# Two matmul accumulator rings re-cut in a two-block transformer kernel, and the side work issued between weight pairs

## The chip, the cores and the metric

The kernel runs as one program on one core of a Trainium2 chip. The metric is the device time of one execution in microseconds (us). Lower is better.

## The reference, cut to what matters

Two transformer blocks follow each other on 512 tokens of width 1024, in float32. The change touches the MLP of the first block, the modulation that is computed beside it for the second block, and, through a shared constant, the start of the MLP of the second block.

```python
# first block
hn = rmsnorm(x, mlp_norm_g)
hid = jnp.square(jax.nn.relu(hn @ w_up))          # 512x1024 @ 1024x4096
x = x + hid @ w_down                              # 512x4096 @ 4096x1024

# second block: six modulation rows of 1024 for x, the first two for ctx too
mod_x = jax.nn.silu(c) @ w_mod + b_mod            # 1x1024 @ 1024x6144
mod_c = jax.nn.silu(c_ctx) @ w_mod + b_mod
h_c = rmsnorm(ctx, g_pre_mix) * (1 + csc1) + csh1
...
y_x = (relu(modulate(x, ...) @ w_mlp_in) ** 2) @ w_mlp_out
```

## The kernel before, in words

**Products.** Every float32 product is made of three matmuls (`mm3`, lines 156 to 158): both factors are split into a high and a low part, and high by high, high by low and low by high are summed in one PSUM bank. ACT makes the high part of a weight tile (L151, a copy of 128x1024), DVE the low part (L152, a subtraction). A weight tile lands in one of two `raw` buffers, and its two parts stand in one of five buffers of each kind.

**The first block's MLP** (`mlp`, called with the name `m1`) runs over four groups of eight hidden slices. In a group, `up` makes eight slices `m1u0` to `m1u31`: 24 matmuls of 512 columns into one bank of the ring `s`, then ACT's relu (L847) and DVE's square (L848) read that bank, and the result is split again. For the first `NSP` = 5 slices the ring has `MORE` banks besides its own, and their matmuls go in two halves of 256 columns. After the eight slices, `token_major` makes the second product for each half of the output columns. Its weights come in four pairs (`m1d000` is group 0, half 0, pair 0), and each of the four token tiles has an accumulator of the ring `a`. DVE adds the finished accumulator to the residual (L987, `xa`). One half is 4 token tiles x 4 pairs x 6 matmuls. The loops stand as pair outside, token tile inside, but the ring `a` has three banks, so the fourth token tile is taken up when the first one's bank has been read.

**Modulation** (`mods`) is a generator whose steps are taken out by `extra`, two at a call. A step of the first kind loads 128x1024 of the modulation weights (`mod`, L897, on SP's queue, two buffers) and adds it, scaled, to an accumulator on DVE (`macc`, L901 and L903): two additions a load for the first two of six column blocks, one for the others. After the eight loads of a block come `MLAG` empty steps, and then a step per row that splits the accumulator, sums it over partitions with four matmuls (`mp`) and writes the row to DRAM. `extra` is called after each `up` and, in the second product, ahead of the addition of each token tile. In the last group its first call takes out what is left and prepares the normalized `ctx`.

**The order** of instructions on each engine is set when the kernel is built. A scheduler goes through the program with estimates of its own, takes the earliest instruction in program order whose inputs and buffers are ready in them, and writes one fixed list for each engine. On the chip each engine works its list in that order. So program order is a priority, and an engine can wait at the head of its list for data that came later than the estimate.

**After the first MLP** `kc` and `vc` are made from `ctx` with the rings `s` and `a`.

**The second block's MLP** (`mlp_seven`, name `m2`) sets `self.rings["s"] = s_banks + list(MORE)` with `s_banks` = `S2` = (5, 6, 7), for its first five slices too. Their first 256 columns need the token tiles 0 and 1 of the normalized input (`h2T`), the other 256 the tiles 2 and 3. `ps` gives out the banks of a ring in turn.

Of the kernel before, what the change touches and what calls it, by code (L numbers as in the profile page):

```python
# [19 lines left out]
NT = SEQ // P  # L20
KC = D // P
FF = 4 * D
NJ = FF // P
# [62 lines left out]
C1 = 0  # L86
KPG = (1, 3)
NSP = 5
MORE = (0, 1)
EARLY = (2, 1)  # L90
A1 = (0, 1, 2)
XR = (3, 5, 7)
# [7 lines left out]
DT = False  # L100
# [6 lines left out]
RB = 1.5  # L107
PBUF = 3
RATIO = 1.6
MLAG = 4  # L110
MRAW = 4
RB_2 = 6
SIZES_2 = (8, 8, 8, 4, 4)
# [20 lines left out]
class Build:  # L134
# [656 lines left out]
                evac(half, t, acc)  # L791
            turns[t], self.last_turn = self.last_turn, None

    def token_major(self, name, nk, weights, moving, evac, in_turn, nt=NT):


        accs = {}

        def part(t, kp, wh, wl):
            if t not in accs:  # L800
                accs[t] = self.ps("a", f"{name}_{t}")
            cols = slice(t * P, (t + 1) * P)
            for i in range(2):
                k = 2 * kp + i
                m = moving(k)
                self.mm3(accs[t], m[:, 0, cols], m[:, 1, cols], wh[:, i, :], wl[:, i, :], k == 0, k == nk - 1)
            if k == nk - 1:
                evac(t, accs[t])

        if in_turn:  # L810
            tiles = [weights(kp) for kp in range(nk // 2)]
            turns = {}
            for t in range(nt):
                for kp in range(nk // 2):

                    behind = turns.get(t - 2) if kp == KB else None
                    with self.tc.issue_after(behind.ins) if behind else nullcontext():
                        part(t, kp, *tiles[kp])
                turns[t], self.last_turn = self.last_turn, None
        else:  # L820
            for kp in range(nk // 2):
                wh, wl = weights(kp)
                for t in range(nt):
                    part(t, kp, wh, wl)

    def mlp(self, hT, w1, w2, evac, extra, name, G=8):

        nc = self.nc
        ac = nc.scalar.activation
        hq = {}  # L830

        def up(j):
            wh, wl = self.weights(f"{name}u{j}", [(0, self.kview(w1, 0, KC, j * P, P))], KC, P)
            acc = self.ps("s", f"{name}up{j}")
            nsp = 2 if j < NSP else 1
            w = SEQ // nsp
            if j % 4 == 0:
                hq[j // 4] = self.hquad(f"{name}hid{j // 4}")
            qd = hq[j // 4]
            for sp in range(nsp):  # L840
                cols = slice(sp * w, (sp + 1) * w)
                for k in range(KC):
                    hqd = hT[k // 4]
                    self.mm3(acc[:, cols], wh[:, k, :], wl[:, k, :], hqd[:, k % 4, 0, cols], hqd[:, k % 4, 1, cols], k == 0, k == KC - 1)
            r = self.ep.tile([P, SEQ], F32, tag="relu", name=f"{name}re{j}", bufs=2)
            s = self.ep.tile([P, SEQ], F32, tag="sqr", name=f"{name}sq{j}", bufs=2)
            ac(out=r, in_=acc, func=AF.Relu)  # L847
            nc.vector.scalar_tensor_tensor(out=s, in0=acc, scalar=0.0, in1=r, op0=ALU.max, op1=ALU.mult)  # L848
            self.split(qd[:, j % 4, 0, :], qd[:, j % 4, 1, :], s)

        s_banks = self.rings["s"]
        self.rings["s"] = s_banks + list(MORE)
        for g in range(NJ // G):
            for j in range(g * G, (g + 1) * G):
                if j == NSP:
                    self.rings["s"] = s_banks
                up(j)
                extra(g)
            for half in range(2):
                def evac_(t, acc):  # L860
                    extra(g)
                    evac(g, half, t, acc)
                self.token_major(f"{name}d{g}{half}", G,
                                 lambda q: self.weights(f"{name}d{g}{half}{q}", [(0, self.kview(w2, g * G + 2 * q, 2, half * 512, 512))], 2, 512),
                                 lambda i: hq[(g * G + i) // 4][:, i % 4], evac_, DT or (g == NJ // G - 1 and half == 1))

    def hquad(self, name):

# [5 lines left out]
    def mods(self):  # L874
# [18 lines left out]
        for cb in range(6):  # L893
# [12 lines left out]

            for _ in range(MLAG):
                yield
# [25 lines left out]
    def dense_one(self):  # L934
        nc, a = self.nc, self.a
        ac = nc.scalar.activation
        x = [self.xp.tile([P, D], F32, tag=f"x{t}", name=f"xa{t}") for t in range(NT)]
        for t in range(NT):
            nc.gpsimd.dma_start(out=x[t], in_=a["x"][0, t * P:(t + 1) * P, :])
        g = self.gp.tile([P, 2, D], F32, tag="g", name="g_mlp")  # L940
        nc.gpsimd.dma_start(out=g[:, 0, :], in_=a["mlp_norm_g"].partition_broadcast(P))
        hT = [self.quad(f"hT{i}") for i in range(2)]

        r2 = self.xc.tile([P, NT], F32, name="r2")

        def evac1(half, t, acc):
            cols = slice(half * 512, half * 512 + 512)
            nc.vector.tensor_tensor(out=x[t][:, cols], in0=acc, in1=x[t][:, cols], op=ALU.add)
            xg = self.ep.tile([P, D], F32, tag="xr", name=f"xg{half}{t}", bufs=2)
            (nc.vector if half else nc.gpsimd).tensor_tensor(out=xg[:, cols], in0=x[t][:, cols], in1=g[:, 0, cols], op=ALU.mult)  # L950
            self.split_T(xg, hT, t, f"n2_{t}", (half,))
            if half == 1:
                self.inv_rms(x[t], r2, t, f"r2_{t}", self.ep.tile([P, D], F32, tag="xr", name=f"xs{t}", bufs=2))
                nc.gpsimd.tensor_tensor(out=r2[:, t:t + 1], in0=r2[:, t:t + 1], in1=r2[:, t:t + 1], op=ALU.mult)
        self.out_proj(a["w_out"], self.mixT, evac1, "o1")

        self.turned_in = self.last_split
        self.banks(a=(0, 1, 2), t=(3, 4), s=(5, 6, 7))

        self.kc = self.xc.tile([P, 4, 2, 256], F32R, name="kc")  # L960
        self.vc = self.xc.tile([P, 2, 2, 512], F32R, name="vc")
        gen = self.mods()
        hcq = []
        seen = set()

        def extra(grp):
            next(gen, None)
            if grp == 3 and 3 not in seen:
                seen.add(3)
                for _ in gen:  # L970
                    pass

                hcq.append(self.ep.tile([P, 8, 2, 256], F32R, tag="xquad", name="hcT", bufs=1))
                hcT = [hcq[0][:, 0:4], hcq[0][:, 4:8]]
                gc = self.columns("g_ctx", (6, 7))
                for t in range(2):
                    cx = self.raw(f"ctx{t}")
                    nc.sync.dma_start(out=cx, in_=a["ctx_2"][0, t * P:(t + 1) * P, :])
                    self.mod_T(cx, gc, hcT, t, f"nc_{t}")
            else:  # L980
                next(gen, None)
        hxT = []
        gx = []

        def evac2(grp, half, t, acc):
            cols = slice(half * 512, half * 512 + 512)
            nc.vector.scalar_tensor_tensor(out=x[t][:, cols], in0=acc, scalar=r2[:, t:t + 1], in1=x[t][:, cols],  # L987
                                           op0=ALU.mult, op1=ALU.add)
            if grp == NJ // 8 - 1 and half == 1:
                if t == 0:  # L990
                    gx.append(self.columns("g_mod1", (0, 1)))
                    hxT.extend(self.quad(f"hxT{i}") for i in range(2))
                nc.gpsimd.dma_start(out=self.xspill[t * P:(t + 1) * P, :], in_=x[t])
                self.mod_T(x[t], gx[0], hxT, t, f"n3_{t}")
        self.mlp(hT, a["w_up"], a["w_down"], evac2, extra, "m1")


        w_in = a["w_in_2"][0]
        hc = hcq[0]
        for i in range(4):  # L1000
            wh, wl = self.weights(f"wkc{i}", [(0, self.kview(w_in, 0, KC, 1024 + i * P, P))], KC, P)
            acc = self.ps("s", f"kc{i}")
            for k in range(KC):
                self.mm3(acc[:, 0:256], wh[:, k, :], wl[:, k, :], hc[:, k, 0, :], hc[:, k, 1, :], k == 0, k == KC - 1)
            self.split(self.kc[:, i, 0], self.kc[:, i, 1], acc[:, 0:256])
        self.early = {(kind, 0): self.weights_two(kind, 0) for kind in EARLY}
        self.token_major("vc", KC, lambda kp: self.weights(f"wvc{kp}", [(0, self.kview(w_in, 2 * kp, 2, 1536, 512))], 2, 512),
                         lambda k: hc[:, k], lambda t, acc: self.split(self.vc[:, t, 0], self.vc[:, t, 1], acc), False, 2)
        return hxT
# [549 lines left out]
```

## Time and profile before

| | |
|---|---|
| median of 3 runs | 1251.21 us (1248.91 to 1252.83) |
| the profiled execution | 1258.43 us, of which the span of instructions is 1256.6 us |
| TensorE (PE) busy | 1210.2 us, 96% of the span |
| VectorE (DVE) busy | 836.8 us, 67% |
| ScalarE (ACT) busy | 593.8 us, 47% |
| mean granted TensorE clock | 0.989 of full speed |

PE is the engine that is nearly always at work, so a change can gain only where PE waits, where its clock is granted at half, or by fewer matmuls. The first block's MLP lies between 278 and 659 us of the span, the start of the second block's MLP at 903 to 940 us.

### The profile page before, as it was taken

Reading aid. Unit: us, or ns where it says so; the run is one execution under the profiler, and the core shown is the slowest. Engines: PE = TensorE matmul, PEld = TensorE weight load, DVE = VectorE, ACT = ScalarE, POOL = GpSimd, SP = SyncE. Lnnn points to the kernel's source line nnn. Section 1 sums busy time; section 2 is a strip of 40 time slices with the busy share of each in tenths; the row PEclk is TensorE's granted clock in tenths of the full one; section 3 lists DMA queues with packets and bytes.
Section 4 is the critical chain, followed back from the end, with each engine's and each line's share of the span. In section 5 each row is a group of like instructions: output and inputs, shape, how many; then the busy total and the mean of one; then the engine's idle time right before and its main releaser. Section 6 shows DMA issues by size and latency. Waiting matters only on the chain. (4 is left out here: it accounts for less than half of the span.)

```text
span 1256.6 us, 16978 instructions
## 1 busy us (share of the span) xinstructions
PE 1210.2 (96%) x6304; PEld 1012.7 (81%) x6304; DVE 836.8 (67%) x1469; ACT 593.8 (47%) x1103; POOL 232.6 (19%) x316
## 2 busy tenths in 40 slices
PE   7898999999999999999999999999999999999997
PEld 6898888789777878888889878777798888888775
DVE  3698776558978758346356557574768568578675
ACT  5576655443324214225245546463666454453442
POOL 2787552220001000000013224130300000000000
PEclk9899999999999999999999999999999999999999
DMA  6222222336658657134145311306554525426331
GB/s 165 64 52 54 66 63 68 101 101 185 201 186 236 214 154 223 62 118 135 67 150 159 85 51 53 102 26 212 157 167 145 164 90 173 146 89 191 106 101 67
DMA packets 154154, 155.42 MB, mean 124 GB/s; under 512 B 14489, under 2 KB 115624, under 8 KB 154072
## 3 DMA queue, kind: packets, MB, share of 16 engines
q1 hardware_dynamic: 149096, 143.08, 37.7%
q0 software_dynamic: 4400, 10.22, 2.8%
q8 instruction: 49, 0.80, 0.3%
q10 hardware_dynamic: 576, 1.05, 0.2%
q14 instruction: 33, 0.27, 0.1%
HBM read 147.96 MB, written 6.36 MB: 123 GB/s over the span
## 5 line engine op out<-in xcount | busy, mean ns | idle before, releaser
L903 DVE SCALAR_TENSOR_TENSOR macc<-mod,silu_c,macc 128x1024 f32<-128x1024 f32 x56 | 70.9, 1279 | 18.3 <-DMA mod<-in_w_mod_dram 18.2
L1461 POOL TENSOR_TENSOR ss<-ss,nhalf 128x1 f32<-128x1 f32 x4 | 2.9, 736 | 335.6 <-DVE ss L1460 335.6
L1313 DVE TENSOR_TENSOR m2d<-m2d,m2d 128x1024 f32<-128x1024 f32 x28 | 34.2, 1222 | 22.8 <-DMA m2d<-in_w_mlp_out_dram 22.6
L928 POOL DMA_DIRECT2D modrows<-mrow x8 | 3.9, 492 | 220.0 <-DVE mrow L926 143.0
L987 DVE SCALAR_TENSOR_TENSOR xa<-m1d,r,xa 128x512 f32<-128x512 f32 x32 | 23.7, 747 | 30.5 <-PE m1d L158 30.5
L151 ACT ACTIVATE m1hid<-m1sq 128x512 fp32r<-128x512 f32 x32 | 20.1, 629 | 40.2 <-DVE m1sq L848 40.1
L152 DVE TENSOR_TENSOR npl<-t,nph 128x512 fp32r<-128x512 f32 x32 | 21.8, 683 | 17.1 <-ACT nph L151 17.0
L185 POOL TENSOR_SCALAR w<-w,g_attn 128x384 f32<-128x384 f32 x20 | 26.1, 1314 | 9.1 <-DMA w<-in_w_in_dram 4.3
L152 DVE TENSOR_TENSOR m1hid<-m1sq,m1hid 128x512 fp32r<-128x512 f32 x32 | 22.0, 687 | 8.4 <-ACT m1hid L151 8.4
L687 DVE TENSOR_REDUCE mb<-sb 128x1 f32<-128x128 f32 (+3 forms) x32 | 15.6, 486 | 16.9 <-PE sb L684 16.8
L1127 ACT ACTIVATE p<-s,m 128x512 f32<-128x512 f32 x32 | 21.9, 687 | 5.6 <-DVE m L1125 5.5
L689 ACT ACTIVATE pb<-sb,mb 128x128 f32<-128x128 f32 (+3 forms) x32 | 16.8, 526 | 16.1 <-DVE mb L687 15.8
L198 POOL TENSOR_SCALAR p<-p,d 128x512 f32<-128x512 f32 x8 | 14.0, 1753 | 53.9 <-DVE d L1128 28.5
L1081 POOL TENSOR_TENSOR tb<-G,nam 128x256 f32<-128x256 f32 x24 | 18.8, 816 | 22.8 <-DVE m L1121 12.3
L151 ACT ACTIVATE nph<-t 128x512 fp32r<-128x512 f32 x32 | 19.0, 595 | 8.1 <-PE t L1138 7.7
L156 PE MATMUL pj<-w_0h,xnT 128*128 128x384 f32 (+1 forms) x48 | 18.1, 377 | 4.9 <-ACT pjs L411 3.7
L848 DVE SCALAR_TENSOR_TENSOR m1sq<-m1up,m1re 128x512 f32<-128x512 f32 x32 | 21.9, 683 | 0.0
L1339 DVE TENSOR_TENSOR y<-m2p,y 128x512 f32<-128x512 f32 x32 | 21.0, 684 | 0.6 <-PE m2p L158 0.6
L1278 ACT ACTIVATE m2sq<-m2up 128x512 f32<-128x512 f32 x32 | 18.6, 581 | 5.3 <-PE m2up L158 5.3
L1280 ACT ACTIVATE m2sq<-m2sq 128x512 f32<-128x512 f32 x32 | 20.2, 632 | 0.9
L151 ACT ACTIVATE pbh<-tb 128x128 fp32r<-128x128 f32 (+3 forms) x32 | 13.8, 434 | 14.5 <-PE tb L707 14.4
L847 ACT ACTIVATE m1re<-m1up 128x512 f32<-128x512 f32 x32 | 18.6, 581 | 3.7 <-PE m1up L158 3.6
(2045 smaller groups left out, 4596.6 us busy)
## 6 DMA issues: line engine op xcount, KB each, us to landing
m2d<-in_w_mlp_out_dram SPq DMA_DIRECT2D x53, 512.0 KB, 3.7
mod<-in_w_mod_dram SPq DMA_DIRECT2D x48, 512.0 KB, 4.2
m1u<-in_w_up_dram SPq DMA_DIRECT2D x32, 512.0 KB, 4.5
m1d<-in_w_down_dram SPq DMA_DIRECT2D x32, 512.0 KB, 4.5
m2u<-in_w_mlp_in_dram SPq DMA_DIRECT2D x32, 512.0 KB, 4.2
w<-in_w_in_dram SPq DMA_DIRECT2D x16, 512.0 KB, 4.0
w<-in_w_in_dram SPq DMA_DIRECT2D x48, 128.0 KB, 2.6
o1w<-in_w_out_dram SPq DMA_DIRECT2D x8, 512.0 KB, 3.8
```

What stands on the lines that cost most here:

```text
L151: self.nc.scalar.activation(out=hi, in_=src, func=AF.Copy)
L152: self.last_split = (eng or self.nc.vector).tensor_tensor(out=lo, in0=src, in1=hi.bitcast(F32), op=ALU.subtract)
L185: eng.tensor_scalar(out=rv[:, i], in0=rv[:, i], scalar1=g, scalar2=None, op0=ALU.mult)
L847: ac(out=r, in_=acc, func=AF.Relu)
L848: nc.vector.scalar_tensor_tensor(out=s, in0=acc, scalar=0.0, in1=r, op0=ALU.max, op1=ALU.mult)
L903: nc.vector.scalar_tensor_tensor(out=accs[s], in0=rw, scalar=sc[:, s, k:k + 1], in1=accs[s], op0=ALU.mult, op1=ALU.add)
L987: nc.vector.scalar_tensor_tensor(out=x[t][:, cols], in0=acc, scalar=r2[:, t:t + 1], in1=x[t][:, cols], op0=ALU.mult, op1=ALU.add)
L1081: nc.gpsimd.tensor_tensor(out=tb[:, h, y], in0=G[:, h, ::-1, o:o + 32][:, :, ::-1], in1=nam[:, y, :].unsqueeze(1).to_broadcast([P, 8, 32]) ...
L1127: ac(out=pr, in_=s, func=AF.Exp, bias=m[:, 2:3], accum_out=den[:, 0:1])
L1280: ac(out=s, in_=s, func=AF.Square)
L1313: tt(out=o, in0=x, in1=z, op=ALU.subtract)
L1339: tt(out=Y[n][tau], in0=acc, in1=Y[n][tau], op=ALU.add)
```

## The change

The ring `a` gets a fourth bank, 5, during the first MLP, and the ring `s` keeps two, 6 and 7. `MORE` becomes (5, 0, 1), so that the first five slices of the first MLP still have five banks. The rings are set back after the MLP. `extra` is called after each weight pair of the second product and no longer ahead of each token tile's addition, and it takes two steps and one step in turn. `MLAG` goes from 4 to 3. The preparation of `ctx` moves to the call of the last group at which the generator has run out.

```diff
-MORE = (0, 1)
+MORE = (5, 0, 1)
...
-MLAG = 4
+MLAG = 3
...
-    def token_major(self, name, nk, weights, moving, evac, in_turn, nt=NT):
+    def token_major(self, name, nk, weights, moving, evac, in_turn, nt=NT, hook=lambda: None):
...
                 for t in range(nt):
                     part(t, kp, wh, wl)
+                hook()
...
             for half in range(2):
-                def evac_(t, acc):
-                    extra(g)
-                    evac(g, half, t, acc)
                 self.token_major(f"{name}d{g}{half}", G,
                                  lambda q: self.weights(f"{name}d{g}{half}{q}", [(0, self.kview(w2, g * G + 2 * q, 2, half * 512, 512))], 2, 512),
-                                 lambda i: hq[(g * G + i) // 4][:, i % 4], evac_, DT or (g == NJ // G - 1 and half == 1))
+                                 lambda i: hq[(g * G + i) // 4][:, i % 4], lambda t, acc: evac(g, half, t, acc),
+                                 DT or (g == NJ // G - 1 and half == 1), hook=lambda: extra(g))
...
-        self.banks(a=(0, 1, 2), t=(3, 4), s=(5, 6, 7))
+        self.banks(a=(0, 1, 2, 5), t=(3, 4), s=(6, 7))
...
-        seen = set()
+        calls = [0]
 
         def extra(grp):
-            next(gen, None)
-            if grp == 3 and 3 not in seen:
-                seen.add(3)
-                for _ in gen:
-                    pass
+
+            calls[0] += 1
+            for _ in range(1 + calls[0] % 2):
+                more = next(gen, "done") != "done"
+            if grp == 3 and not more and not hcq:
 
                 hcq.append(self.ep.tile([P, 8, 2, 256], F32R, tag="xquad", name="hcT", bufs=1))
...
                     self.mod_T(cx, gc, hcT, t, f"nc_{t}")
-            else:
-                next(gen, None)
...
         self.mlp(hT, a["w_up"], a["w_down"], evac2, extra, "m1")
+        self.banks(a=(0, 1, 2), t=(3, 4), s=(5, 6, 7))
```

## Rows read from the trace of the kernel before

**Rows 1.** The page, busy time of each engine: us, share of the span, instructions.
```profile
PE 1210.2 (96%) x6304; PEld 1012.7 (81%) x6304; DVE 836.8 (67%) x1469; ACT 593.8 (47%) x1103; POOL 232.6 (19%) x316
```
**Rows 2.** Waits of PE, 270 to 700: total us, times, longest.
```profile
PE m1d L156 <- DVE xa L987: 4.9, 3, 2.4
PE m1up L158 <- DVE m1u8l L152: 1.9, 1, 1.9
```
**Rows 3.** Timeline of PE, 344 to 444: start, us, what, [idle before].
```profile
344.16 0.50 PE L156 MATMUL m1d<-m1d000h,m1hid 128*128 128x512 f32 x1 [0.97 <-DVE xa L987]
...
369.25 0.50 PE L156 MATMUL m1d<-m1d010h,m1hid 128*128 128x512 f32 x1 [1.50 <-DVE xa L987]
...
440.15 0.40 PE L158 MATMUL m1d<-m1d103h,m1hid 128*128 128x512 f32 x1
442.96 0.68 PE L156 MATMUL m1d<-m1d100h,m1hid 128*128 128x512 f32 x1 [2.41 <-DVE xa L987]
443.44 0.63 PE L157 MATMUL m1d<-m1d100l,m1hid 128*128 128x512 f32 x1
```
**Rows 4.** Windows: busy us (x) of PE, PEld, DVE, ACT, POOL; PEclk, DMA, GB/s.
```profile
440.50:444.30 3.80, 1.39 (x5) 1.06 (x5) 2.91 (x3) 0.00 (x0) 0.00 (x0) 0.84 0.61 174
904.00:908.50 4.50, 2.61 (x18) 2.61 (x18) 4.33 (x7) 2.12 (x8) 3.66 (x7) 0.87 0.69 198
```
**Rows 5.** Timeline of DVE, 440 to 449.
```profile
440.96 1.28 DVE L903 SCALAR_TENSOR_TENSOR macc<-mod,silu_c,macc 128x1024 f32<-128x1024 f32 x1 [1.64 <-DMA mod<-in_w_mod_dram]
442.16 0.74 DVE L987 SCALAR_TENSOR_TENSOR xa<-m1d,r,xa 128x512 f32<-128x512 f32 x1
...
447.48 0.75 DVE L987 SCALAR_TENSOR_TENSOR xa<-m1d,r,xa 128x512 f32<-128x512 f32 x1
```
**Rows 6.** Tiles macc and mod: durations ns min/median/max, first and last start.
```profile
L903 DVE SCALAR_TENSOR_TENSOR macc<-mod,silu_c,macc x56: 1262/1282/1293, 287.5 to 501.2; 128x1024 f32<-128x1024 f32 x56
...
L897 SPq DMA_DIRECT2D mod<-in_w_mod_dram x48: 327/340/441, 240.3 to 495.9; - x48
```
**Rows 7.** The same windows, over slices of groups 0 and 1.
```profile
290.54:325.46 34.92, 34.92 (x223) 31.57 (x222) 32.94 (x36) 13.38 (x19) 0.48 (x1) 1.00 0.58 180
...
378.85:423.70 44.85, 44.85 (x193) 36.40 (x194) 37.52 (x41) 18.31 (x24) 6.21 (x11) 1.00 0.80 243
```
**Rows 8.** Timeline of PE: the last matmul of slices 13 and 21.
```profile
412.19 0.39 PE L158 MATMUL m1up<-hT,m1u13l 128*128 128x512 f32 x1
...
507.68 0.39 PE L158 MATMUL m1up<-hT,m1u21l 128*128 128x512 f32 x1
507.91 0.40 PE L156 MATMUL m1up<-hT,m1u22h 128*128 128x512 f32 x1
```
**Rows 9.** Timeline of DVE: the square that frees the banks of the same slices.
```profile
421.02 0.68 DVE L848 SCALAR_TENSOR_TENSOR m1sq<-m1up,m1re 128x512 f32<-128x512 f32 x1
...
510.12 0.68 DVE L848 SCALAR_TENSOR_TENSOR m1sq<-m1up,m1re 128x512 f32<-128x512 f32 x1
```
**Rows 10.** Timeline of ACT, 418 to 420.
```profile
418.78 1.06 ACT L151 ACTIVATE m1d102h<-m1d 128x1024 fp32r<-128x1024 f32 x1 [4.17 <-DMA m1d<-in_w_down_dram]
```
**Rows 11.** Timeline of PE, 655: the first `kc` matmul.
```profile
655.32 0.28 PE L156 MATMUL kc<-hcT,wkc0h 128*128 128x256 f32 x1
```
**Rows 12.** Timeline of PE, 905 to 924: the start of the second MLP.
```profile
905.89 0.39 PE L157 MATMUL m2up<-h2T,m2u1h 128*128 128x256 f32 x1 [1.89 <-DVE h2T L152]
...
917.79 1.03 PE L220 MATMUL n_3t<-ident,n_3x 128*128 128x128 f32 x8
...
923.64 0.28 PE L156 MATMUL m2up<-h2T,m2u4h 128*128 128x256 f32 x1
923.76 0.28 PE L157 MATMUL m2up<-h2T,m2u0h 128*128 128x256 f32 x1
```
**Rows 13.** Timeline of DVE, 914 to 922: the input of token tile 3.
```profile
914.63 0.74 DVE L236 TENSOR_SCALAR n_3x<-xb,ssx 128x1024 f32<-128x1024 f32 x1
...
920.62 1.29 DVE L152 TENSOR_TENSOR h2T<-n_3v,h2T 128x512 fp32r<-128x512 f32 x2 [0.40 <-ACT h2T L151]
```

## The prediction

> **What bounds the kernel now.** I read the page first: PE is busy for 96% of the span and the next engine, DVE, for 67% [rows 1]. So time can come only from PE's idle stretches, its half-clock stretches, or PE work saved; the change saves no PE work. Next I read PE's own waits in the stretch of the first MLP [rows 2]. There are two kinds: three waits of 4.9 us for the addition `xa` of a token tile, and one of 1.9 us for the low part of a weight tile, `m1u8l`. The timeline shows where the three are [rows 3]: always at the first `m1d` matmul of a half's fourth token tile, which takes the bank of the first tile. The first tile's last matmul lies 12 matmuls ahead of that point, about 437.4 for the third wait, and its addition ends at 442.90 [rows 5]: 5.5 us later, though the addition takes 0.74. What stands before it on DVE is a modulation step, itself waiting 1.64 us for its load [rows 5]. In program order two such steps stand ahead of each addition, so they go first, and DVE works its list in order.
>
> The wait for `m1u8l` has the same root. As the fourth token tile runs after the other three, it needs all four weight pairs again, so four of the five weight buffers stay taken until the half ends, and the next slices' weights are split late.
>
> **What can be won.** The page's idle times begin at a matmul's end, and matmuls overlap: one of 512 columns starts 0.23 us after the one before [rows 8], though each is shown with 0.40. Start to start the third wait is 442.96 - 440.15 - 0.23 = 2.58 us where 2.41 is shown. So I add 0.17 to each of the four: 6.8 + 0.7 = 7.5 us. After the third wait the granted clock is 0.84 over 3.8 us [rows 4], so part of it is at 1.2 GHz, and the matmuls follow at 0.48 and about 0.43 us instead of 0.23 [rows 3]; six of them make 1.2 us. In all 8.7 us can be won, from nothing (the waits only move) to all of it.
>
> **Part 1: four banks for the second product.** No tile of a half waits for another; each pair is used for all four tiles and its buffers come free every 24 matmuls (5.6 us). This takes away the three waits' cause and the late weights. What is late next: the next half's first tile takes the first tile's bank, wanted 19 matmuls (4.4 us) after that tile's last matmul, instead of 13 (3.0 us). Bounds: with additions at once it costs nothing; with the additions as late as now, the third tile's, which ends at 448.23 for a last matmul at 440.15 [rows 5, 3], misses its 4.4 us by 3.7. I take 0.8 us over the boundaries, nearer to nothing, because the new program order puts all four additions ahead of the steps of the last pair; only steps of earlier pairs whose loads came late can stand before them.
>
> **Part 2: modulation's steps.** The work is the same: 48 loads, 56 additions of 1.28 us and 8 openings [rows 6]. The generator has 81 steps now and is emptied at two a call; with `MLAG` 3 it has 75 at one and a half, so loads per call go from 48/81 x 2 = 1.19 to 0.96, 19% fewer. The last load, now at 495.9 [rows 6], belongs to the last call of group 2. That matters where DVE is busy 32.94 of 34.92 us, and where it is busy 37.52 of 44.85 with 243 GB/s of DMA [rows 7]. On SP's queue a modulation load that waits for one of its two buffers holds the weight loads behind it; fewer of them between weights bring these earlier. `MLAG` itself I cost at nothing: a row's four matmuls wait for no accumulator now [rows 2]. If they did, PE would pay one late load, of the size of the 1.64 us in [rows 5]. The `ctx` part moves from the first to the third call of group 3, at nothing too: its reader `kc` starts at 655 [rows 11], a second product away; without that cover `kc` would wait for the two slices (11 us) by which it moves.
>
> **Part 3: two banks for the slices.** This is the new risk. Slice j+2 takes slice j's bank. Between lies one slice of 24 matmuls, so the bank is wanted 25 matmuls, 5.8 us, after slice j's last matmul has started; with three banks it was 11.4 us. The lag from that start to the end of the square is 510.80 - 507.68 = 3.1 us at its least and 421.70 - 412.19 = 9.5 at its greatest [rows 8, 9]. The great one is in-order waiting: ACT waited 4.17 us for a weight tile of the second product [rows 10], and the relu of slice 13 stood behind it. A lag L over 5.8 costs (L - 5.8)/2 a slice, as two banks return in turn. Bounds: nothing at 3.1; at 9.5 for the six reusing slices of group 1, 11.1 us. I take the middle of the two rows, L = 6.3, and so 6 x 0.5/2 = 1.6 us: the weights come free evenly and the loads are fewer, so the late weight of [rows 10] should grow rare, but DVE stays well loaded there. The Trainium skill (Perfetto Trace Analysis, Optimizing Tensor Performance) wants independent matmul groups to rotate through PSUM banks so that the evacuation of one overlaps the matmuls of the next. By that rule two banks are enough at 3.1 us and Part 3 costs nothing; at the lag of [rows 9] in group 1 the overlap fails, and the sum would carry up to the 11.1 us.
>
> After the MLP the first `kc` takes bank 5, now that of the last token tile. It runs inside the tail of `m1d` today [rows 11]. `kc` 1 and 2 have banks of their own and can go first, so it costs nothing if their weights are there, 24 matmuls at 0.12 us (2.8) if not; I take 0.6.
>
> **Part 4: the second block's MLP.** `MORE` = (5, 0, 1) is joined to `S2` = (5, 6, 7) there, so its first five slices take banks 5, 6, 7, 5, 0: slice 3 must wait until slice 0 is whole and read. Now the first halves of all five slices run while token tiles 2 and 3 are prepared; they last until 923.76 [rows 12], and four matmuls of second halves (0.5 us) stand among them. The input of tile 3 is ready at 920.62 + 1.29 = 921.91 [rows 13], so 1.85 us of cover is left. Slice 3's first half is 24 x 0.118 = 2.8 us of it. Without it PE is through at 923.76 - 0.5 - 2.8 = 920.4 and waits 1.5 us. Bounds: nothing, if the transposes `n_3t` move up, since they run at 917.79 with their input ready at 915.37 [rows 12, 13]; 4.3 us, if slice 4 does not come ahead of slice 3 either. I take 1.5. A wait of 1.89 us lies just before, and over it the clock is granted at 0.87 [rows 4], 1.2 us at half clock; I add half of that price, 0.6. Slice 5 also takes bank 5, right after slice 3, but slice 6 has another bank and can go first.
>
> **The sum.** 8.7 - 0.8 - 1.6 - 0.6 - 2.1 = 3.6 us won. The profiled execution, 1258.43 us (1256.6 of span and 1.8 around it), would become 1254.8; it lies 7.2 us above the median of the runs, to which I carry the difference: 1251.2 - 3.6 = 1247.6 us.
>
> **Rivals.**
> - Clean: the lags stay under 5.8 and 4.4 us, and the transposes move up. Then 8.7 less about 1 is won: 1243.5 us. For it speaks 3.1 us in group 2 [rows 8, 9], against it DVE's load in groups 0 and 1 [rows 7].
> - The wait only moves, so the change does not do what it says: modulation steps of earlier pairs still stand before the additions, as in [rows 5]. A half's end then costs 3.7 and 1.2 for the clock in place of 0.8: 8.7 - 4.9 - 1.6 - 0.6 - 2.1 = -0.5, or 1251.7 us.
> - Slower: two banks starve PE in group 1. With the other terms 5.2 us are won, so it decides from (L - 5.8) x 3 = 5.2, a mean lag of 7.5 us. At the 9.5 of [rows 9] it costs 11.1: 1251.2 + 5.9 = 1257.1 us. For it speaks [rows 10], against it that a stalled PE lets DVE and ACT catch up. The Trainium skill (TensorE: Matmul & The Clock Gate, A second HAM failure mode) tells of a kernel that cycled through PSUM banks with short idles and whose clock went back and forth; if each of the six stalls here cost the 1.2 us of half clock, this rival would stand at 1264. The trace agrees in part: the clock fell at the idle of 2.41 us [rows 4], while after those of 0.97 and 1.50 us the first matmul shows 0.50 us, not 0.68 [rows 3].
>
> **How the numbers follow.** 0.3% is 3.75 us, about what a measurement of this kernel can tell from no change. Chances: forecast 0.50 (its sum lies at that edge, so 0.22 faster and 0.28 same); clean 0.20, all faster; moved 0.15 (0.12 same, 0.03 slower); starved 0.15 (0.12 slower, 0.03 same). That makes faster 0.42, same 0.43, slower 0.15. The forecast's own range is 1244.5 to 1250.5. The whole range goes from the clean case, 1243.5, to 1254.0, half-way between the moved and the starved case; about 0.1 is left out at either end.
>
> **What would show it.** Right: no wait of PE for `xa` within a half, and under 1 us at the ends of halves; the wait for `m1u8l` gone; the last `mod` load near the end of group 2; a wait of one to two us at the first second-half matmul of `m2up`, with slice 3 after slices 0, 1, 2. Wrong: waits of `m1up` for `m1sq` of over 4 us in all (two banks are too few), `xa` lags over 4.4 us (the steps still come first), or no second wait in `m2up`. The most fragile step is L = 6.3: the scheduler's new lists decide it, and the trace of before cannot show them.

## The result, and the profile after

The changed kernel takes 1259.91 us in the median of 6 runs (1257.48 to 1262.73), the kernel before 1251.22 us beside it. The ratio is 1.0067, with a 95% interval of 1.0051 to 1.0082: 0.67% slower, 8.4 us. The forecast was 1247.6 us with a range to 1254.0, so the time lies outside it, on the other side of no change. Measured once more beside other kernels the ratio was 1.0044 [1.0025, 1.0063]. The profiled execution took 1262.73 us, 1261.0 of them span.

PE is busy for 1214.1 us with the same 6304 matmuls, before for 1210.2 [rows 1]; this line of the page doesn't say where the time went:

```profile
PE 1214.1 (96%) x6304; PEld 1012.4 (80%) x6304; DVE 835.9 (66%) x1469; ACT 595.5 (47%) x1103; POOL 230.3 (18%) x316
```

The waits of PE between 270 and 700 us say more (total us, times, longest):

```profile
PE m1d L156 <- DVE xa L984: 2.1, 1, 2.1
PE nc_1t L220 <- ACT nc_0v L245: 1.2, 1, 1.2
PE m1up L156 <- ACT m1u27h L151: 1.1, 1, 1.1
PE m1up L158 <- DVE m1u27l L152: 0.5, 1, 0.5
PE vc L157 <- DVE wvc0l L152: 0.5, 1, 0.5
PE nc_1t L220 <- DVE nc_0v L247: 0.5, 1, 0.5
PE x L156 <- DVE vc L152: 0.3, 1, 0.3
PE vc L156 <- ACT wvc0h L151: 0.2, 1, 0.2
PE vc L157 <- DVE wvc2l L152: 0.2, 1, 0.2
```

Of the two rows that the change was to remove [rows 2], the three waits of 4.9 us for `xa` have become one of 2.1, and the wait for `m1u8l` is gone. No row names `m1sq`: the slices never wait for one of their two banks. But new rows have come, first around `ctx` (`nc_0v`, `nc_1t`) and slice 27, then around `vc` and `x`. The windows show the same by stretch (busy us of PE, PEld, DVE, ACT, POOL; then granted clock, DMA share, GB/s):

```profile
276.00:560.00 284.00, 281.86 (x1331) 232.31 (x1330) 200.57 (x215) 87.83 (x108) 15.27 (x27) 1.00 0.58 178
560.00:610.00 50.00, 46.59 (x198) 36.78 (x198) 28.93 (x40) 25.45 (x40) 3.84 (x7) 0.97 0.39 116
574.00:583.00 9.00, 5.71 (x23) 3.89 (x21) 8.22 (x16) 7.61 (x16) 1.04 (x2) 0.82 0.62 174
```

PE is idle for 2.1 of the 284 us in which the change was to gain, and for 3.4 of the next 50, part of them at a granted clock of 0.82.

**Where the time went.** The start of the first slice moves by up to 4 us between profiles of kernels that are alike up to there, so I count from it. The table gives, for every kernel of this study, how much longer (+) or shorter (-) than before each stretch took in its profile, from the ends of these last matmuls: of slice 24 (`m1u24`), of slice 28, of the first MLP (`m1d313`), of the second attention's products of `x` with `w_1`, and of `m2w050` early in the second MLP. Before, the stretches last 291.84, 24.04, 64.41, 179.24 and 130.06 us. Behind the last mark all agree within 0.1 us.

| us against before | to slice 24 | slices 25-28 | rest of MLP | `kc`, `vc`, attention two | to `m2w050` | time against before, by runs |
|---|---|---|---|---|---|---|
| changed kernel | -7.4 | +7.1 | -1.3 | +7.2 | +0.6 | 1.0067 [1.0051, 1.0082] |
| the same again | -6.3 | +7.0 | -1.3 | +3.7 | +0.5 | 1.0044 [1.0025, 1.0063] |
| ctx_own | -7.5 | +0.1 | -0.2 | +5.3 | -1.0 | 1.0003 [0.9989, 1.0018] |
| ctx_scratch | -7.0 | +1.0 | -1.2 | +3.4 | -1.2 | 0.9991 [0.9977, 1.0004] |
| vc_ring | -7.1 | +7.0 | -1.2 | +1.1 | -1.0 | 1.0021 [1.0003, 1.0039] |
| m2_more | -8.4 | +7.7 | -1.3 | +3.2 | -1.4 | 1.0037 [1.0022, 1.0051] |
| all_three | -8.3 | +0.1 | -0.2 | -0.1 | -1.6 | 0.9970 [0.9954, 0.9987] |
| vc_apart | -6.8 | +0.1 | -0.2 | +2.7 | -1.7 | 0.9981 [0.9965, 0.9996] |
| b_banks | -8.3 | 0.0 | -1.3 | +2.1 | -1.5 | 0.9943 [0.9926, 0.9960] |
| banks_apart | -8.6 | 0.0 | -1.3 | +1.0 | -1.6 | 0.9963 [0.9949, 0.9977] |
| place_only | -9.1 | 0.0 | -1.3 | +3.0 | +0.2 | 0.9955 [0.9939, 0.9971] |
| pace_only | -9.3 | +12.2 | -1.3 | +0.9 | -1.5 | 1.0052 [1.0034, 1.0071] |
| steps_early | -8.2 | +13.2 | -1.3 | +3.2 | -1.6 | 1.0072 [1.0056, 1.0089] |
| b_reset | -1.3 | 0.0 | 0.0 | +1.0 | -1.7 | 1.0017 [0.9997, 1.0038] |
| b_more | -1.4 | 0.0 | 0.0 | +1.2 | -1.0 | 1.0007 [0.9990, 1.0024] |

Two kinds of matmul only change sides of a mark. Where the last modulation row is late, its four `mp` matmuls (0.9 us) run behind slice 24: in the changed kernel, its repairs, pace_only and steps_early. And ten `kc` matmuls (1.2 us) run ahead of the end of the first MLP before, in b_reset and in b_more, and behind it in all others: that is the -1.3 of the third column, and it comes back in the fourth. (In the three rows with -0.2 there, eight transposes of `ctx` have come over from the second column.)

The last two rows tell how far one profile can be trusted: these kernels leave the first MLP as it was, and still show -1.3 and -1.4 up to slice 24. The waits of [rows 2] were that much longer than usual in the profile of before. In the column of attention two single profiles of kernels whose rings stand alike differ by 3 us and more; only their mean, or the runs, can be read.

So of the -7.4 and -6.3 us up to slice 24, 1.3 is chance in the profile of before, and 0.9 is the four matmuls that run later. The change won 4 to 5 us there, near what it was to win, and lost it again in three places.

**The first loss: `ctx` in group 3.** The timeline of the changed kernel from 542 to 580 us, four engines in one list (start, us, what, [idle before]):

```profile
542.82 9.88 SPq L977 DMA_DIRECT2D ctx<-in_ctx_dram  x2
567.23 0.68 DVE L921 TENSOR_TENSOR mrow<-mp,mrow 1x512 f32<-1x512 f32 x1 [3.33 <-PE mp L920]
569.14 1.21 DVE L925 SCALAR_TENSOR_TENSOR mrow<-mrow,grow 1x1024 f32<-1x1024 f32 x1
570.38 1.06 ACT L260 ACTIVATE nc_0x<-ctx 128x1024 f32<-128x1024 f32 x1 [1.21 <-DVE mrow L925]
573.27 6.85 SPq L173 DMA_DIRECT2D m1u<-in_w_up_dram  x3
575.61 0.66 PE L220 MATMUL nc_1t<-ident,nc_1x 128*128 128x128 f32 x4 [1.16 <-ACT nc_0v L245]
576.73 0.66 PE L220 MATMUL nc_1t<-ident,nc_1x 128*128 128x128 f32 x4 [0.46 <-DVE nc_0v L247]
577.41 1.06 ACT L151 ACTIVATE m1u27h<-m1u 128x1024 fp32r<-128x1024 f32 x1 [0.82 <-DMA m1u<-in_w_up_dram]
578.52 0.50 PE L156 MATMUL m1up<-hT,m1u27h 128*128 128x512 f32 x1 [1.14 <-ACT m1u27h L151]
579.78 0.76 PE L158 MATMUL m1up<-hT,m1u27l 128*128 128x512 f32 x1 [0.53 <-DVE m1u27l L152]
```

The two `ctx` tiles are loaded at 542.8 and 552.4 us into the two `raw` buffers, those through which every weight passes. They are read from 570.38 on, and the row says what ACT waited for: `mrow`, the last modulation row. `mod_T` squares `ctx` into a scratch tile (`nc_0x`) that comes from the same pair of buffers as the rows (`mrow`, `grow`), and that pair is free only when the last row has been made. Until then both `raw` buffers are taken. The weights of slice 27 are asked for at 573.27, split at 577.41, and PE stands still. In the kernel before, the last row was begun at 536.2, and `ctx`, loaded at 547.3, was read at 551.0, as soon as it had landed (the tiles `mrow` and `nc_0x` before: durations in ns, first and last start):

```profile
L926 DVE SCALAR_TENSOR_TENSOR mrow<-mrow,grow x5: 1201/1205/1207, 376.5 to 536.2; 1x1024 f32<-1x1024 f32 x5
L260 ACT ACTIVATE nc_0x<-ctx x1: 1065/1065/1065, 551.0 to 551.0; 128x1024 f32<-128x1024 f32 x1
```

**The second loss: the rings behind the MLP.** The products `x` of the second attention take banks 0 and 1 in turn. A view of the tile `x` between 660 and 712 us (line, count: duration in ns, first and last start), before and then in the changed kernel:

```profile
L156 PE MATMUL x<-hxT,w_0h x48: 279/281/385, 671.2 to 702.0; 128*128 128x256 f32 x48
```

```profile
L156 PE MATMUL x<-hxT,w_0h x48: 279/281/387, 682.2 to 699.0; 128*128 128x256 f32 x48
```

The first `x` product starts at 682.2, after the last matmul of `vc`, while before it started at 671.2, among those of `vc`. The line that sets the rings back makes the ring `a` start at bank 0. In the kernel before, the ring had been left standing at bank 2. So `vc` takes 0 and 1 now, both banks that `x` wants; before it took 2 and 0, and one of the two was free.

**The third loss** is small, half a microsecond in the second MLP, and told with Part 4 below.

### The profile page after: what moved, and what is told of

It reads as the page before. It is cut to its first block, busy times and chain, and to the rows that moved or that the text cites. A ratio compares the mean times of both kernels' runs of the same rounds, so it can differ in the third digit from the quotient of the medians.

```text
span 1261.0 us, 16979 instructions
## 1 busy us (share of the span) xinstructions
PE 1214.1 (96%) x6304; PEld 1012.4 (80%) x6304; DVE 835.9 (66%) x1469; ACT 595.5 (47%) x1103; POOL 230.3 (18%) x316
## 5 line engine op out<-in xcount | busy, mean ns | idle before, releaser
L1119 DVE CUSTOM_DVE_ANT_0 s<-s,tb 128x256 f32<-128x256 f32 x32 | 13.6, 426 | 16.8 <-PE s L158 16.7
L152 DVE TENSOR_TENSOR ml<-macc,mh 128x1024 fp32r<-128x1024 f32 x8 | 9.7, 1225 | 18.9 <-ACT mh L151 18.9
```

The costliest lines, as they stand in the source:

```text
L152: self.last_split = (eng or self.nc.vector).tensor_tensor(out=lo, in0=src, in1=hi.bitcast(F32), op=ALU.subtract)
```

## The experiments

Theory: the banks give what they were to give, and what is lost comes from (T1) `ctx`, (T2) the rings' start, (T3) the second MLP's extra banks. Rival: the new lists cost something everywhere, and undoing single lines won't give the time back. The first three runs undo one thing each, the fourth all three.

**ctx_own**

```diff
-                    cx = self.raw(f"ctx{t}")
+                    cx = self.ep.tile([P, D], F32, tag="mraw", name=f"ctx{t}", bufs=2)
```

> The changed kernel, with ctx loaded into the two buffers of the modulation weights (free by then) instead of the two raw buffers of the MLP's weights. Theory 1 (the ctx part, moved next to the last modulation row, holds both raw buffers until its scratch tile comes free, so that slice 27's weights are loaded late): the idle stretch and the half clock at slice 27, about 6 us together, go; some 1254 us where the changed kernel has 1260. Rival (the loss lies in the two-bank ring or the new step order): within 1 us of the changed kernel.

Measured: 1.0003 [0.9989, 1.0018], 0.4 to 0.6% below the changed kernel. The stall is gone; the window holds no idle time:

```profile
560.00:610.00 50.00, 50.00 (x225) 40.54 (x224) 30.92 (x43) 26.49 (x42) 4.17 (x7) 1.00 0.31 96
```

By the table the slices 25 to 28 and the rest of the MLP take 5.9 us less than in the changed kernel (7.1 - 1.3 against 0.1 - 0.2). T1 is the largest loss.

**vc_ring**, behind the first MLP:

```diff
-        self.banks(a=(0, 1, 2), t=(3, 4), s=(5, 6, 7))
+        self.banks(a=(2, 0, 1), t=(3, 4), s=(5, 6, 7))
```

> The changed kernel, with the ring a set to (2, 0, 1) after the MLP and not to (0, 1, 2), which is how it stood in the kernel before; vc then takes banks 2 and 0 and not 0 and 1, which are the two banks of the next stage's projections. Theory 2 (the reset ring blocks the first projection until vc has been read, attention starts late and PE pays in the second block's attention): 5 to 6 us come back, some 1254 us, and the first x projection starts before vc ends. Rival (attention's loss is an effect of the ctx part's delay, or chance): the projection moves, the time stays within 1 us of the changed kernel.

Measured: 1.0021 [1.0003, 1.0039], 0.2 to 0.5% or 3 to 6 us below the two measurements of the changed kernel; with the second of them the intervals overlap. `x` starts at 667.5 again, among `kc` and `vc`:

```profile
L156 PE MATMUL x<-hxT,w_0h x48: 279/281/390, 667.5 to 702.3; 128*128 128x256 f32 x48
```

**m2_more**, in the second MLP:

```diff
-        self.rings["s"] = s_banks + list(MORE)
+        self.rings["s"] = s_banks + [0, 1]
```

> The changed kernel, with the second MLP's five early banks back at (5, 6, 7, 0, 1). Theory 3 (slice 3 of the second MLP shares bank 5 with slice 0): 0.7 us come back by the trace (0.17 us of idle and the later order), at most the 2.1 of the prediction; 1258 to 1259 us. Rival (the doubled bank is a main part of the loss): over 3 us come back.

Measured: 1.0037 [1.0022, 1.0051], 0.1 to 0.3% below the changed kernel, with intervals that touch or overlap, so the runs don't show T3. Its stretch to `m2w050` is 2.0 us shorter than in the changed kernel, but most of that is the clock, as told at the end.

**all_three** makes these three edits at once.

> The changed kernel with all three edits. Theories 1 to 3 together: the gain of the first two groups of the MLP stays, about 6 to 8 us, and nothing is given back: 1244 to 1247 us, below the kernel before. Rival (two-bank ring or step order cost by themselves): at or above the kernel before, 1251 us or more.

Measured: 0.9970 [0.9954, 0.9987]. The single repairs give 0.4 to 0.6, 0.2 to 0.5 and 0.1 to 0.3%, together 0.7 to 1.0, and with them the change is a gain. As it was put, the rival falls: undoing single lines gives the time back. But the gain of 0.30% is only about half of the 6 to 8 us that were expected, and b_banks below stands another 0.27% lower. So a part of the rival stays; the end of the next section comes back to it.

**after_again**

> The changed kernel once more, beside the three that follow, so that they have their own measure of it. Expected 0.5 to 0.8% above the kernel before, as in its first runs (1.0067).

Measured: 1.0044 [1.0025, 1.0063], so the loss lies between 0.4 and 0.7%. It ran beside the next three, which start from the kernel before and add one part of the change each.

**b_banks**: the first MLP's banks alone; the three places stand in that MLP, ahead of it and behind it, where the rings are put back to where they stood.

```diff
-        self.rings["s"] = s_banks + list(MORE)
+        self.rings["s"] = s_banks + [5, 0, 1]
...
-        self.banks(a=(0, 1, 2), t=(3, 4), s=(5, 6, 7))
+        self.banks(a=(0, 1, 2, 5), t=(3, 4), s=(6, 7))
...
+        self.banks(a=(2, 0, 1), t=(3, 4), s=(5, 6, 7))
```

> The kernel before with the first MLP's banks alone: four for the token tiles, two and the three extra ones of the first pairs for the slices; modulation's steps, MLAG and the end of the list stay as before, and behind the MLP the rings are put back to where the kernel before has them; the second MLP is that of before. Theory (the banks carry the gain, two banks for the slices cost nothing, and the loss comes from the ctx part, the rings behind the MLP and the second MLP): the waits for xa within a half are gone, PE's idle in the first MLP falls from 6.8 to under 3 us, no wait for m1sq, and the time is 4 to 8 us (0.3 to 0.6%) below before. Rival (the gain needs the steps between the weights): the additions still stand behind two steps of modulation, the waits move to the ends of halves, idle stays at 5 us or more, time within 0.2% of before. Rival (two banks starve PE without the new steps): waits for m1sq of over 4 us, time above before.

Measured: 0.9943 [0.9926, 0.9960], the fastest kernel of the study, 7.1 us below before. The waits of PE between 270 and 700 us:

```profile
PE x L158 <- DVE w_1l L152: 0.8, 1, 0.8
PE s L156 <- ACT kT L151: 0.7, 1, 0.7
PE m1up L156 <- DVE m1sq L848: 0.6, 1, 0.6
```

In the first MLP one wait of 0.6 us for a slice's bank is left, and none for `xa`, though modulation's steps still stand ahead of the additions.

**b_reset**

```diff
         self.mlp(hT, a["w_up"], a["w_down"], evac2, extra, "m1")
+        self.banks(a=(0, 1, 2), t=(3, 4), s=(5, 6, 7))
```

> The kernel before with one line more: behind the first MLP the rings are set to start at banks 0, 1, 2. Theory (the ring's start is a loss of its own, as vc then takes both banks of the second attention's x projection): vc and x come as in the changed kernel, x starts only after the last vc, PE's idle between 660 and 790 us grows by about 1 us, and the time rises by 2 to 5 us (0.15 to 0.4%). Rival (the ring's start only goes along with the late ctx): within 0.1% of before.

Measured: 1.0017 [0.9997, 1.0038]. The middle is 2.1 us, as the theory's lower end; the interval also holds no change.

**b_more**, in the second MLP:

```diff
-        self.rings["s"] = s_banks + list(MORE)
+        self.rings["s"] = s_banks + [5, 0, 1]
```

> The kernel before with the second MLP's extra banks alone: 5, 0, 1 in place of 0, 1. Prediction's step: a second wait at the first matmul of a second half, 1.5 us and 0.6 of clock, so 2.1 us (0.17%) slower. Rival from the trace of the changed kernel, where that wait was 0.17 us: 0.65 us, under 0.1%. Rival from the run with MORE undone: 0.3%, 3.7 us, slower.

Measured: 1.0007 [0.9990, 1.0024], 0.9 us. The 3.7 us are excluded, and the 2.1 of the prediction lie near the end of the interval.

**ctx_scratch**: is it the scratch that holds `ctx`, or are two `raw` buffers too few?

```diff
-                    self.mod_T(cx, gc, hcT, t, f"nc_{t}")
+                    self.mod_T(cx, gc, hcT, t, f"nc_{t}", tiles=(self.ep.tile([P, D], F32, tag="mraw", name=f"nc_{t}x", bufs=2), "v"))
```

> The changed kernel with one thing moved: the scratch in which a ctx tile is scaled and normed comes from the pair of buffers in which modulation's weights arrived, not from the pair that the modulation rows also use; the two ctx tiles still arrive in the buffers of the weights (raw). Theory (ctx holds both raw buffers because its scratch waits for the last modulation row, and m1u27's weights come late for that): ctx is read soon after it has landed, m1u27's load is issued some 15 us earlier, slice 27 doesn't stop PE, idle between 560 and 610 us falls from 3.4 to under 0.5, and the time falls by 4 to 6 us (0.3 to 0.5%), as it did when ctx had buffers of its own. Rival (two raw buffers are too few for ctx and a stream of weights, however early ctx is read): slice 27 or a neighbour still stops PE for 2 us or more, time within 0.15% of the changed kernel.

Measured: 0.9991 [0.9977, 1.0004], 0.5 to 0.8% below the changed kernel. `ctx` still passes through `raw`, and is now read as soon as it has landed (timeline of ACT):

```profile
547.70 1.06 ACT L260 ACTIVATE nc_0x<-ctx 128x1024 f32<-128x1024 f32 x1 [0.71 <-DMA ctx<-in_ctx_dram]
```

The last row comes no earlier than in the changed kernel (the tile `mrow`, durations in ns, first and last start), but nothing waits for it:

```profile
L925 DVE SCALAR_TENSOR_TENSOR mrow<-mrow,grow x5: 1202/1205/1207, 381.1 to 571.4; 1x1024 f32<-1x1024 f32 x5
```

So it is the shared scratch, not the number of `raw` buffers.

**vc_apart** and **banks_apart** give `vc` banks that the attention's `x` doesn't want, in all_three and in b_banks:

```diff
-        self.banks(a=(2, 0, 1), t=(3, 4), s=(5, 6, 7))
+        self.banks(a=(2, 5), t=(3, 4), s=(6, 7))
```

> The changed kernel with the three repairs (ctx in buffers of its own, the second MLP's extra banks 0 and 1, the rings behind the first MLP), the last of them in another form: vc takes banks 2 and 5, kc and the rest 6 and 7, so that banks 0 and 1 are free for the second attention's x. Theory (what counts is that x finds a free bank): x starts before the last vc and the time is at or below the one of that kernel, 0.995 to 0.997 of before. Rival (fewer banks for kc and s cost more): 0.998 or above.

> The kernel with the first MLP's banks alone (0.9943 of before), and vc on banks 2 and 5, kc and the rest on 6 and 7 behind the MLP. If what counts is that x finds a free bank, 0.993 to 0.995 of before; if fewer banks for kc and s cost more, 0.996 or above.

Measured: 0.9981 [0.9965, 0.9996] and 0.9963 [0.9949, 0.9977]. Both middles lie above those of the kernels that they start from, with intervals that overlap, and both fall where fewer banks for `kc` and `s` were to cost more. With the overlap that is not shown either; a gain is not seen.

**steps_early** is b_banks with the new steps (place, pace, `MLAG`); what is left of them is taken out at the first call of group 3. Against the changed kernel, beside the rings and extra banks of all_three:

```diff
-            if grp == 3 and not more and not hcq:
+            if grp == 3 and not hcq:
+                for _ in gen:
+                    pass
```

> The kernel with the first MLP's banks alone (0.9943 of before), and to it the new steps of modulation: between the weights, three in two calls, MLAG 3; what is left of them is emptied at the first call of group 3, so that ctx comes there as in the kernel before. Theory (the steps' place and pace are worth nothing, and all that the change could win is the banks): within 0.2% of that kernel, so 0.992 to 0.996 of before. Rival (the new steps delay the additions or the rows): PE's waits for xa come back as in the changed kernel, 1.5 to 3 us, and the time is 0.2 to 0.4% above it, 0.996 to 0.998, where the run with all three repairs stood. Rival (they help): under 0.992.

Measured: 1.0072 [1.0056, 1.0089]. Both the theory and the rivals were wrong on the size: the new steps cost 1.3% on top of the banks. PE's waits:

```profile
PE nc_0t L220 <- DVE nc_0x L236: 5.7, 1, 5.7
PE m1d L156 <- DVE xa L986: 1.1, 2, 0.6
```

As `ctx` now stands early in program order, its transposes stand in PE's list ahead of slice 25, and PE itself waits 5.7 us for the scratch that waits for the last row. It is T1 again, with PE in the place of the weights. Up to slice 24 the new steps cost only about 1 us: -8.2 against -8.3, with 0.9 of the -8.2 for the row's four matmuls that run later. What was open is which part of the edit makes the row late: that gave the last two.

**place_only** is b_banks with the steps between the weights (`hook` in `token_major`, after a pair), two at each call, `MLAG` 4.

```diff
+                hook()
...
-                def evac_(t, acc):
-                    extra(g)
-                    evac(g, half, t, acc)
```

> The kernel with the first MLP's banks alone, and modulation's steps between the weights, two at each call as before, MLAG 4. Theory (it is the pace that makes the last row late, and the place is worth nothing): the last row is done in group 2, no wait for nc_0x, idle between 560 and 610 us under 0.5, time 0.992 to 0.996 of before. Rival (the place does it): PE waits for nc_0x or for a weight tile of slices 25 to 27 by 3 us or more, time above 1.0.

**pace_only** is b_banks with the steps ahead of the additions, three in two calls, and `MLAG` 3.

```diff
-MLAG = 4
+MLAG = 3
...
-            else:
+            elif calls[0] % 2:
                 next(gen, None)
```

> The kernel with the first MLP's banks alone, and modulation's steps ahead of the additions as before, but three in two calls and MLAG 3; what is left is emptied at the first call of group 3. Theory (the pace does it): the last row ends after 555 us, PE waits for nc_0x by 4 to 7 us, time 1.003 to 1.008 of before. Rival (the place does it): 0.992 to 0.997.

Measured: 0.9955 [0.9939, 0.9971] and 1.0052 [1.0034, 1.0071]. With the new place alone the last row of `place_only` is begun at 519.2 us and no wait is left in the first MLP:

```profile
L925 DVE SCALAR_TENSOR_TENSOR mrow<-mrow,grow x5: 1202/1206/1207, 365.5 to 519.2; 1x1024 f32<-1x1024 f32 x5
```

With the new pace and `MLAG` 3 alone it is begun at 561.6, and PE waits as in steps_early:

```profile
L926 DVE SCALAR_TENSOR_TENSOR mrow<-mrow,grow x5: 1203/1204/1212, 379.2 to 561.6; 1x1024 f32<-1x1024 f32 x5
```

```profile
PE nc_0t L220 <- DVE nc_0x L236: 5.7, 1, 5.7
```

The pace does it. At the old pace the place gains and costs nothing that the runs can tell (0.9955 against 0.9943).

## Why the prediction was wrong, point by point

**What can be won: right.** 8.7 us less Parts 1 and 3 were to leave 6.3; up to slice 24 the two profiles of the changed kernel are 7.4 and 6.3 us shorter, 6.5 and 5.4 without the four matmuls that run later. About 1.3 of this, as of the 8.7, was chance in the one profile that I read, as b_reset and b_more show. With the banks alone the runs give 7.1 us (b_banks).

**Part 1: the mechanism right, the handover too cheap.** No wait for `xa` stands within a half, and the late weights of [rows 2] are gone. At the ends of halves I took 0.8 us; the trace has one wait of 2.06, and in the second profile two of 2.6 us together. What is late there is not a modulation step of an earlier pair, as I had thought, but the last weight pair. DVE's timeline, and PE's wait:

```profile
439.41 1.23 DVE L152 TENSOR_TENSOR m1d113l<-m1d,m1d113h 128x1024 fp32r<-128x1024 f32 x1 [2.54 <-ACT m1d113h L151]
440.55 2.72 DVE L984 SCALAR_TENSOR_TENSOR xa<-m1d,r,xa 128x512 f32<-128x512 f32 x4
441.35 0.50 PE L156 MATMUL m1d<-m1d110h,m1hid 128*128 128x512 f32 x1 [2.06 <-DVE xa L984]
```

All four additions stand behind the split of `m1d113`, which itself waited 2.54 us for ACT's half. It is the in-order waiting of [rows 5], with a weight in the place of a step. This wait comes with the new steps and not with the banks alone. All nine profiles of kernels with both the new place and the new pace have it, 1.1 to 2.6 us in total. Of the four kernels with the new banks and not both of these (b_banks, banks_apart, place_only, pace_only) none has it.

**Part 2: the loads right, the step that failed is "The `ctx` part moves ... at nothing too".** The last `mod` load came at 518.1 us, at the end of group 2 as said. But I costed `ctx` by its reader `kc`, which was indeed 80 us away, and not by what `ctx` holds while it waits: the two `raw` buffers, a scratch that the modulation rows also use, and a place in PE's list. Fewer steps a call make the last row late (569 us for 536), the scratch waits for the row, and the weights wait for `ctx`. It is the late row and not the later call: in pace_only and steps_early `ctx` comes at the first call, as before, and the loss is greater. In the changed kernel it cost 5.9 us in the profiles and 0.4 to 0.8% by the runs, as ctx_own and ctx_scratch show; that the pace brings it is shown by the square of b_banks, place_only, pace_only and steps_early. `MLAG` was tried only together with the pace, and place and pace only with the new banks. That fewer loads bring the weights earlier is worth nothing here: b_banks has the old pace, and is the fastest.

**Part 3: mis-sized, 1.6 us for nothing.** The profile of the changed kernel has no wait for `m1sq`, others have one of 0.2 to 0.6. Both terms of the cost were off. The lag L, taken at 6.3 us, is 4.7 on the mean of the six reusing slices of group 1 in that profile, 6.2 at most. And I had held the distance from one use of a bank to the next at one slice of 24 matmuls, 5.8 us; there it is 6.0 to 8.0. In every kernel with the new banks the second product of a group begins before its slices end, in all four groups, and in none of the three without them (before, b_reset, b_more). Its matmuls stand between the slices (timeline of PE):

```profile
411.82 0.40 PE L158 MATMUL m1up<-hT,m1u14l 128*128 128x512 f32 x1
412.06 0.40 PE L158 MATMUL m1d<-m1d100h,m1hid 128*128 128x512 f32 x1
...
413.71 0.39 PE L158 MATMUL m1d<-m1d100h,m1hid 128*128 128x512 f32 x1
413.94 0.40 PE L156 MATMUL m1up<-hT,m1u15h 128*128 128x512 f32 x1
```

Eight of them, 1.9 us, stand between slices 14 and 15, and eight more of that pair's 24 between slices 12 and 13. Whether the four banks or the two bring this is not shown. By the rule of the Trainium skill that I had set against the row (Perfetto Trace Analysis, Optimizing Tensor Performance: independent groups rotate through banks, so that one's evacuation overlaps the next one's matmuls) Part 3 was to cost nothing, and the trace agrees.

**Behind the MLP: a step that was missing.** I had looked at `kc` and bank 5 (0.6 us; no wait for it is seen) and not at where the ring `a` stands afterwards. The mean of the column of attention two is +4.0 us over the six kernels whose ring starts at 0, 1, 2, and +1.4 over the eight where it starts at 2 (with before, 0, and without the two of banks 2 and 5), so T2 is worth some 2.5 us, 0.2%. The runs give 0.2 to 0.5% in the changed kernel and 0.17% [-0.03, 0.38] in the kernel before. That it costs in the changed kernel is shown by its two measurements taken together; its size is not settled, and how the late `x` costs more in the attention behind it was not followed.

**Part 4: mis-sized, 2.1 us for 0.5.** Slice 3 does come late, slice 4 ahead of it, and the second wait is there, at the first matmul of a second half:

```profile
924.26 0.39 PE L156 MATMUL m2up<-h2T,m2u0h 128*128 128x256 f32 x1 [0.17 <-ACT h2T L151]
924.49 0.28 PE L156 MATMUL m2up<-h2T,m2u1h 128*128 128x256 f32 x1
924.61 0.28 PE L156 MATMUL m2up<-h2T,m2u2h 128*128 128x256 f32 x1
924.73 0.28 PE L156 MATMUL m2up<-h2T,m2u4h 128*128 128x256 f32 x1
924.99 0.39 PE L157 MATMUL m2up<-h2T,m2u0h 128*128 128x256 f32 x1
```

But it is 0.17 us, for I had taken DVE's low part of `h2T` as what it waits for [rows 13]. The first matmul of each slice wants only ACT's high part, which is earlier, and the first ones of four slices fill the time until the low part is there. The column to `m2w050` gives the price: of the kernels whose clock stays up there, ctx_own, ctx_scratch, vc_ring and b_more, with bank 5, stand at -1.0 to -1.2, and the eight without it at -1.4 to -1.7, half a microsecond apart.

**The sum and the rivals.** In the changed kernel's first profile the stretches add up to -7.4 + 5.8 + 7.2 + 0.6 = +6.2 us, in the second to -6.3 + 5.7 + 3.7 + 0.5 = +3.6; the runs say +8.4 and +5.5. The slower rival gave 1257.1 us, near the measured time, but by luck: its mechanism did not come, and no slice starved. The half-clock stretches that I had added to it stayed away with its stalls. The Trainium skill's rule on cycling banks (TensorE: Matmul & The Clock Gate, A second HAM failure mode) had nothing to act on here.

**What stays open.** all_three stands 0.27% (3.4 us) above b_banks, vc_apart 0.18% above banks_apart. They differ in the steps' place and pace and in where `ctx` lies. The profiles show about 1 us of it: up to slice 24 both stand at -8.3 in the table, but 0.9 of all_three's is the row's four matmuls that run later, and it has the wait of Part 1, which b_banks has not (waits of PE between 270 and 700 us):

```profile
PE m1d L156 <- DVE xa L984: 1.3, 2, 0.9
```

The rest is not found.

## What to carry to other kernels

A tile that is wanted late is not free to move: cost it by the buffers, scratch and queue places it holds from its load to its read, and ask what must come first before it can be read. When side work is slowed down so that the main work flows, look at what its last piece releases. And where a ring of banks is re-cut for one stage, its position behind that stage is part of the edit: set it back to where it stood, not to its beginning.

## What the hardware showed unexpectedly

The clock does not follow the length of a stall alone. At the start of the second MLP PE waits 1.80 us for `h2T` in the changed kernel and 1.81 in m2_more, in both after three matmuls of 256 columns behind the same projection. Windows of 9.5 us, which begin 1.2 us before these three in the changed kernel and 0.8 in m2_more, in this order:

```profile
906.00:915.50 9.50, 7.70 (x47) 7.25 (x46) 7.42 (x12) 5.23 (x15) 5.13 (x10) 0.82 0.85 268
```

```profile
903.00:912.50 9.50, 7.69 (x62) 7.31 (x61) 7.51 (x13) 5.68 (x17) 5.40 (x11) 1.00 0.87 277
```

In one the clock is granted at 0.82, part of the stretch at 1.2 GHz, and 47 matmuls fit; in the other it stays at 2.4 GHz, and 62 fit. That is the 1.6 us by which before, the two profiles of the changed kernel and place_only stand apart from their like in the last stretch of the table (before, the second profile and place_only fit 48 or 49 matmuls at 0.82 into such a window, ctx_own, all_three and b_reset 62 or 63 at 1.00). At this place the sixteen profiles of the study have waits of 1.6 to 1.9 us; the clock fell in these four, after 1.7 to 1.9, and stayed in twelve, after 1.6 to 1.8. I had priced the clock after Part 4's second wait from it, at 0.6 us. In pace_only the clock was at 1.2 GHz throughout the 6 us that begin with the end of the wait of 5.7 us:

```profile
566.00:572.00 6.00, 4.83 (x18) 3.47 (x18) 3.20 (x6) 3.61 (x8) 0.73 (x2) 0.50 0.62 175
```
